# Seven-product blocks in a new order, with two of the sums of each step made by accumulating transfers

## The chip, the cores and the metric

The kernel runs on one core of a Trainium2 chip. The metric is the time of one execution in microseconds on the device; the median of the runs is given. The profile is one execution, taken by the hardware profiler.

## The reference

Two layers work on 256 tokens of width 2048, all in float32. Each layer does, in short:

```
h = rms_norm(x, norm1_g);  z = h @ w_in            # 2048 x 3584: gating u, v; queries, keys, values
A = gating of u by a causal 128 x 128 mixing of v   # 16 channel groups
B = attention in a window of 128, with sinks        # 16 query heads, 4 key/value heads
x = x + concat(rms_norm(A), rms_norm(B)) @ w_out
h2 = rms_norm(x, norm2_g)
x = x + (silu(h2 @ w_gate) * (h2 @ w_up)) @ w_down  # inner width 5632
```

## The kernel before

Every product is made in float32 accuracy from three passes of a faster format: a weight buffer of 128 x 1024 (two slabs of 512 columns, 512 KB, tag `raw`, eight buffers) is loaded from the sync engine's queue, ScalarE casts it to `wh` (five buffers), VectorE makes the remainder `wl = raw - wh` (four buffers), and TensorE multiplies high by high, high by low and low by high (`split2` and `mm3`; lines 123, 124 and 159 to 161). The activations are the stationary side, split once in the same way (`pairs`, `ext`).

An ordinary unit (`unit`) takes one weight buffer to two accumulators of 128 tokens each: twelve matmuls. Most of the feed-forward part's gate and up products (10 of 11 column blocks of 512 in each layer) and the queries are made otherwise, by seven products in place of eight on a 2 x 2 arrangement (`seven`). For the gate and up blocks its rows are the two parities of the inner slabs and its columns are gate and up; for the queries the columns are the two halves. The text writes b11, b12, b21 and b22 for the four weight buffers of a quarter i (i from 0 to 3), and p:i for product p in quarter i: one split and six matmuls into one of five PSUM banks, a half-step. Products 1 and 2 take b11 and b21 plainly; 5 takes b11 + b12, 6 takes b11 + b12 + b22 (`t2`), 3 takes b22, 7 takes b12 + b22, and 4 takes t2 + b21. A block is 28 half-steps.

In the kernel before, the numbers in `bank` are 0 for products 1 and 2, 1 for 5, 3 for 6, 4 for 3 and 2 for 7 and 4. A quarter loads b11, b12 and b22 at once. VectorE adds b12 onto b11 (line 365) and makes t2 (line 366). The sum b12 + b22 is made by VectorE (line 372) or, for the quarters in `by_dma`, by a transfer that GpSimd issues and that adds b22 from memory onto the buffer (line 368). The sum t2 + b21 is always such a transfer (line 374). After the four quarters, bank 0 is copied out and m0 = bank 3 + bank 0 is formed (lines 391 and 392); then come 2:0 to 2:3, with b21 loaded a second time, and 4:0 to 4:3 on the kept t2. Small sums between them (line 396) form c21, c12 and c22, and line 400 puts c21 back into bank 2. `out` then makes the gated activation of each token half (lines 1058 and 1059), which is transposed (`act_T`) for the down product.

The order of the work is the order of the Python calls, with delays counted by `tick`; a planner then orders each engine's instructions and assigns buffers. In the feed-forward part of a layer `s_stream` runs the ten blocks one after the other and yields 300 times (`HALVES`). Beside it, `std_stream` runs ordinary units: 88 of the down product and 16 of the one block that is not done by seven products. Five of them go first (`FF_FIRST`), then they are spread evenly over the yields, and 16 (`TAIL`) remain after the last block. The first layer's queries run beside the key/value, gating and first u products of that layer: `q_to` takes 30 steps of `q["steps"]` in a pace set by the ordinary units; the second layer's run beside the end of the first layer's feed-forward part and the start of the second layer.

Of the kernel before, what the change touches and what calls it, by code (L numbers as in the profile page):

```python
# [12 lines left out]
F32 = mybir.dt.float32  # L13
# [57 lines left out]
EXT_AT = (6.5, 8, 11, 13, 16, 18, 21.5, 24)  # L71
MASK_AFTER = ((5, 5), (4, 4))
GATE_LOAD = ((24, 29), (5, 15))
PARTS = (
    "a0 a0 a1 a1 s a0 a0 s a1 s a1 s s s b0 s b0 s b0 s b0 s b1 s b1 s b1 s b1 s b2 b2 b2 b2 b3 b3 b3 b3",
    "a0 a0 a1 a1 a0 a0 s a1 a1 s b0 b0 s b0 s b0 s s b1 s b1 s b1 s b1 s s b2 s b2 s b2 b2 s b3 b3 b3 b3",
# [14 lines left out]
def trunk(ctx, tc, x, xt, w_in, w_q, w_out, w_oa, w_uh, w_gate, w_up, w_down, sgu_w, sgu_g, consts,  # L91
# [66 lines left out]
    def mm3(acc, ah, al, wh, wl, first, last, again=False):  # L158
        nc.tensor.matmul(acc, ah, wh, start=first, stop=False, skip_group_check=again)  # L159
        nc.tensor.matmul(acc, ah, wl, start=False, stop=False, skip_group_check=again)  # L160
        nc.tensor.matmul(acc, al, wh, start=False, stop=last, skip_group_check=again)  # L161
# [171 lines left out]
    def seven(src, pairs, ext, out, end=lambda sg: None, soon=False, by_dma=(), put_off=False):  # L333
        bank = [pa.tile([P, NB], F32, tag="acc", name=f"m{i}") for i in range(5)]

        def s_unit(raw, m, i, op, first, last):
            wh, wl = split2(raw)
            for j in range(2):
                ah, al = (op(2 * i + j, h) for h in range(2))
                mm3(  # L340
                    bank[m], ah, al, wh[:, j, :], wl[:, j, :], first and j == 0,
                    last and j == 1, m in (0, 2),
                )
            tick(0.5)

        def a_op(k, t):
            return lambda p, h: pairs[p][:, h, k, t * P : (t + 1) * P]

        def e_op(n):
            return lambda p, h: ext[p][:, h, n, :]  # L350

        kept = []
        before = []
        for i in range(4):
            b11 = raw_load(src(0, 0, i))
            b12 = raw_load(src(0, 1, i))
            b22 = raw_load(src(1, 1, i))
            t2 = ap.tile([P, 2, NB], F32, tag="spt", name="t2", bufs=4)
            first, last = i == 0, i == 3
            s_unit(b11, 0, i, a_op(0, 0), first, last)  # L360
            yield
            if soon and first:
                s_unit(b22, 4, i, e_op(3), first, last)
                yield
            nc.vector.tensor_tensor(b11, b11, b12, ALU.add)  # L365
            nc.vector.tensor_tensor(t2, b11, b22, ALU.add)  # L366
            if i in by_dma:
                nc.gpsimd.dma_start(b12, src(1, 1, i), accum_op=ALU.add)
            s_unit(b11, 1, i, e_op(1), first, last)
            yield  # L370
            if i not in by_dma:
                nc.vector.tensor_tensor(b12, b12, b22, ALU.add)
            s_unit(t2, 3, i, e_op(2), first, last)
            anchor[0] = nc.gpsimd.dma_start(t2, src(1, 0, i), accum_op=ALU.add)  # L374
            yield
            if before:
                s_unit(*before.pop())
                yield
            if not (soon and first):
                s_unit(b22, 4, i, e_op(3), first, last)  # L380
                yield
            kept.append(t2)
            if put_off and i in by_dma and not last:
                before.append((b12, 2, i, e_op(0), first, last))
                continue
            s_unit(b12, 2, i, e_op(0), first, last)
            yield
        m0, c12, c21, c22 = (
            zp.tile([P, NB], F32, tag="z", name=v) for v in ("m0", "c12", "c21", "c22")
        )  # L390
        nc.scalar.copy(m0, bank[0])
        nc.vector.tensor_tensor(m0, bank[3], m0, ALU.add)
        yield

        def add(out, x, y):
            nc.vector.tensor_tensor(out, x, y, ALU.add)

        steps = {
            0: lambda: add(c21, bank[2], m0),
            1: lambda: (nc.scalar.copy(bank[2], c21), add(c12, bank[1], m0)),  # L400
            2: lambda: (add(c22, bank[1], c21), add(c12, bank[4], c12)),
            5: lambda: out(0, bank[0], m0, c12),
        }
        for i in range(8):
            if i < 4:
                s_unit(raw_load(src(1, 0, i)), 0, i, a_op(1, 0), False, i == 3)
            else:
                s_unit(kept[i - 4], 2, i - 4, a_op(1, 1), False, i == 7)
            yield
            steps.get(i, lambda: None)()  # L410
        later(1, lambda: out(1, bank[2], c21, c22))
        end([m0, c21])
        yield

    def seven_low(src, pairs, ext, done, tag="hT"):
        def half(raw, acc, op, i, first=False, stop=False):
            wh, wl = split2(raw)
            for j in range(2):
                ah, al = (op(2 * i + j, h) for h in range(2))
                mm3(  # L420
                    acc, ah, al, wh[:, j, :], wl[:, j, :], first and i + j == 0,
                    stop and i + j == 2, not first,
                )
            tick(0.5)

        def a_op(k, t):
            return lambda p, h: pairs[p][:, h, k, t * P : (t + 1) * P]

        def e_op(n):
            return lambda p, h: ext[p][:, h, n, :]  # L430

        def bank(name):
            return pa.tile([P, NB], F32, tag="acc", name=name)

        def held(name):
            return tp.tile([P, 2, NB], F32, tag=tag, name=name)

        x, y, s = [], [], []
        acc0 = bank("l0")
        for i in range(2):  # L440
            x.append(raw_load(src(0, 0, i)))
            y.append(held("ys"))
            nc.sync.dma_start(y[i], src(0, 1, i))
            b22 = raw_load(src(1, 1, i))
            s.append(held("ss"))
            half(x[i], acc0, a_op(0, 0), i, True, True)
            nc.vector.tensor_tensor(x[i], x[i], y[i], ALU.add)
            nc.vector.tensor_tensor(s[i], x[i], b22, ALU.add)
            anchor[0] = nc.gpsimd.dma_start(y[i], src(1, 1, i), accum_op=ALU.add)
            yield  # L450
        acc1 = bank("l1")
        nc.scalar.copy(acc1, acc0)
        for i in range(2):
            half(s[i], acc1, e_op(2), i, False, True)
            anchor[0] = nc.gpsimd.dma_start(s[i], src(1, 0, i), accum_op=ALU.add)
            yield
        mp = wp.tile([P, 2, NB], F32, tag="raw", name="mp", bufs=8)
        nc.scalar.copy(mp[:, 0], acc1)
        acc2 = bank("l2")
        for i in range(2):  # L460
            half(y[i], acc2, e_op(0), i, True, True)
            yield
        nc.scalar.copy(mp[:, 1], acc2)
        for i in range(2):
            half(raw_load(src(1, 0, i)), acc0, a_op(1, 0), i, False, True)
            yield
        done[0, 0](acc0, None)
        for i in range(2):
            half(x[i], acc1, e_op(1), i, False, True)
            yield  # L470
        done[1, 1](acc1, mp[:, 1])
        for i in range(2):
            half(s[i], acc2, a_op(1, 1), i, False, True)
            yield
        done[0, 1](acc2, mp[:, 0])
        for i in range(2):
            half(raw_load(src(1, 1, i)), acc1, e_op(3), i, False, True)
            yield
        done[1, 0](acc1, None)

    def q_product(lay, pairs, ext):
        q = {"k": 0}
        q["steps"] = seven(
            lambda r, c, i: w_q[lay, c, i, r], pairs, ext, lambda *a: q["out"](*a),
            soon=True, by_dma=range(4 if lay == 0 else 0),
        )
        return q

    def q_to(q, share):
# [32 lines left out]
    for lay in range(L):  # L522
# [526 lines left out]
        def act_later(b, sg, held=held, release=release):  # L1049
            for c in range(2):  # L1050
                def ready(c=c):
                    held.append((b, c, sg))
                    release()

                later(2 + c, ready)
# [3 lines left out]
            nc.vector.scalar_tensor_tensor(sg, c, nrstd2[t], sg, ALU.mult, ALU.mult)  # L1059

        def s_block(b, lay=lay, pairs2=pairs2, ext2=ext2, gated=gated, act_later=act_later):
            return seven(
                lambda r, c, i: (w_gate, w_up)[c][lay, b, i, r], pairs2, ext2, gated,
                lambda sg: act_later(b, sg), soon=b == S_BLOCKS[0], by_dma=(0, 2), put_off=True,
            )

        seven_done = [False]

        def s_stream(s_block=s_block):
            for b in S_BLOCKS:  # L1070
                yield from s_block(b)

        seeds = []
        left = [NFF]
# [230 lines left out]
```

## Time and profile before

| | |
|---|---|
| time, median of 3 runs | 1907.09 us (1906.76 to 1910.26) |
| profiled execution | 1906.77 us, its span 1905.1 us |
| TensorE (PE) busy | 1892.9 us, 8624 matmuls and transposes |
| VectorE (DVE) busy | 1745.5 us |
| ScalarE (ACT) busy | 1374.7 us |
| GpSimd (POOL) busy | 183.9 us |
| transfers | 463.12 MB, mean 243 GB/s |

In the profile, a row of a group names the line, the engine, the operation, what is written and what is read with their shapes, the count, the busy time, the mean of one instruction and the idle time of the engine ahead of it with what ended it. PE is the matmuls, PEld the weight loads that run beside them, SPq the sync engine's transfer queue. Matmuls are pipelined and overlap in the record: one lasts 0.39 us, while the next starts earlier.

### The profile page before, as it was taken

The numbers are of one execution on the slowest core, as the hardware profiler recorded it, in microseconds if no ns is written. First come the engines' busy times: TensorE is split into PE (matmuls) and PEld (weight loads), VectorE is DVE, ScalarE is ACT, GpSimd is POOL, SyncE is SP. The second block draws the span as 40 slices with busy tenths as digits, with TensorE's granted clock in tenths as the row PEclk, the third lists the DMA queues.
The fourth block names the chain that finished last, engine by engine and source line by source line (L and its number), as shares of the span: only waits on it lengthen the run. The fifth ranks groups of instructions, "written<-read, shape, count | busy, mean of one in ns | idle before, by whom it ended". The sixth has DMA issues, their size and how long they took to land.

```text
span 1905.1 us, 25218 instructions
## 1 busy us (share of the span) xinstructions
PE 1892.9 (99%) x8624; PEld 1544.2 (81%) x8624; DVE 1745.5 (92%) x1894; ACT 1374.7 (72%) x1860; POOL 183.9 (10%) x184
## 2 busy tenths in 40 slices
PE   9999999999999999999999999999999999999999
PEld 6887788888888888888888778888888888888887
DVE  7988989999999999999798888999999999999993
ACT  8668777677767776777776886766877677676774
POOL 0231001000100001000002200000000100010000
PEclk9999999999999999999999999999999999999999
DMA  9973668888977897889578648697789788888783
GB/s 356 261 284 133 194 202 243 248 247 276 271 238 245 270 290 228 243 261 290 185 217 291 191 153 237 212 280 224 233 282 288 227 254 264 270 249 251 249 277 110
DMA packets 129153, 463.12 MB, mean 243 GB/s; under 512 B 14336, under 2 KB 14720, under 8 KB 129024
## 3 DMA queue, kind: packets, MB, share of 16 engines
q1 hardware_dynamic: 105840, 378.54, 53.9%
q0 software_dynamic: 22464, 81.80, 23.7%
q8 instruction: 67, 1.10, 0.2%
q10 hardware_dynamic: 720, 1.18, 0.2%
q14 instruction: 62, 0.51, 0.1%
HBM read 459.36 MB, written 2.10 MB: 242 GB/s over the span
## 4 chain that ended last, share of the span: by engine, by line
PE 94%; ACT 2%; DVE 2%; issue 1%; DMA 0%; POOL 0%; SPq 0%; DVEq 0%; ACTq 0%; POOLq 0%
PE m L160 15%; PE m L159 15%; PE m L161 15%; PE dacc L160 11%; PE dacc L159 11%; PE dacc L161 11%; PE acc L160 4%; PE acc L161 3%; PE acc L159 3%; PE l L159 1%; PE l L160 1%; PE l L161 1%; PE ps_f L242 1%; PE ps_n L242 1%; DVE wl L124 1%
## 5 line engine op out<-in xcount | busy, mean ns | idle before, releaser
L123 ACT CAST wh<-raw 128x1024 fp32r<-128x1024 f32 (+1 forms) x794 | 814.0, 1050 | 366.5 <-DVE raw L365 165.7
L124 DVE TENSOR_TENSOR wl<-raw,wh 128x1024 fp32r<-128x1024 f32 (+1 forms) x794 | 943.9, 1217 | 83.0 <-issue 25.5
L159 PE MATMUL m<-wh,ext 128*128 128x512 f32 x704 | 276.7, 393 | 0.0
L160 PE MATMUL m<-wl,ext 128*128 128x512 f32 x704 | 275.0, 391 | 0.0
L161 PE MATMUL m<-wh,ext 128*128 128x512 f32 x704 | 274.4, 390 | 0.0
L160 PE MATMUL dacc<-wl,aT 128*128 128x512 f32 x624 | 243.5, 390 | 0.0
L159 PE MATMUL dacc<-wh,aT 128*128 128x512 f32 x624 | 243.0, 391 | 0.0
L161 PE MATMUL dacc<-wh,aT 128*128 128x512 f32 x624 | 242.9, 389 | 0.0
L124 DVE TENSOR_TENSOR wl<-t,wh 128x1024 fp32r<-128x1024 f32 x176 | 213.1, 1221 | 10.0 <-issue 5.2
L123 ACT CAST wh<-t 128x1024 fp32r<-128x1024 f32 x176 | 184.3, 1051 | 37.0 <-DVE t L366 14.1
L159 PE MATMUL m<-wh,hT 128*128 128x512 f32 x528 | 206.3, 391 | 0.0
L160 PE MATMUL m<-wl,hT 128*128 128x512 f32 x528 | 205.7, 390 | 0.0
L161 PE MATMUL m<-wh,hT 128*128 128x512 f32 x528 | 205.5, 389 | 0.0
L160 PEld LDWEIGHTS m<-wl,ext 128*128 128x128 f32 x704 | 132.2, 188 | 29.1 <-DVE wl L124 2.2
L159 PEld LDWEIGHTS m<-wh,ext 128*128 128x128 f32 x704 | 132.2, 188 | 27.6 <-ACT wh L123 0.8
L161 PEld LDWEIGHTS m<-wh,ext 128*128 128x128 f32 x704 | 132.1, 188 | 27.5
L159 PEld LDWEIGHTS dacc<-wh,aT 128*128 128x128 f32 x624 | 117.1, 188 | 25.0 <-ACT wh L123 0.7
L160 PEld LDWEIGHTS dacc<-wl,aT 128*128 128x128 f32 x624 | 117.2, 188 | 24.7 <-DVE wl L124 0.6
L161 PEld LDWEIGHTS dacc<-wh,aT 128*128 128x128 f32 x624 | 117.1, 188 | 24.2
L374 POOL DMA_DIRECT2D t<-in_w_gate_dram x80 | 69.1, 864 | 525.0 <-DVE wl L124 412.9
L161 PEld LDWEIGHTS m<-wh,hT 128*128 128x128 f32 x528 | 99.1, 188 | 20.6
L159 PEld LDWEIGHTS m<-wh,hT 128*128 128x128 f32 x528 | 99.1, 188 | 20.3
(212 smaller groups left out, 2907.5 us busy)
## 6 DMA issues: line engine op xcount, KB each, us to landing
raw<-in_w_gate_dram SPq DMA_DIRECT2D x176, 512.0 KB, 5.9
raw<-in_w_up_dram SPq DMA_DIRECT2D x176, 512.0 KB, 5.9
raw<-in_w_down_dram SPq DMA_DIRECT2D x176, 512.0 KB, 5.8
t<-in_w_gate_dram POOLq DMA_DIRECT2D x80, 512.0 KB, 7.7
raw<-in_w_in_dram SPq DMA_DIRECT2D x68, 512.0 KB, 6.7
raw<-in_w_out_dram SPq DMA_DIRECT2D x48, 512.0 KB, 4.3
raw<-in_w_up_dram POOLq DMA_DIRECT2D x40, 512.0 KB, 6.5
raw<-in_w_q_dram SPq DMA_DIRECT2D x32, 512.0 KB, 5.7
```

The source lines that it names most:

```text
L123: nc.scalar.copy(wh[:, j : j + step, :], src)
L124: last_wl[0] = nc.vector.tensor_tensor(wl[:, j : j + step, :], src, f(wh[:, j : j + step, :]), ALU.subtract)
L159: nc.tensor.matmul(acc, ah, wh, start=first, stop=False, skip_group_check=again)
L160: nc.tensor.matmul(acc, ah, wl, start=False, stop=False, skip_group_check=again)
L161: nc.tensor.matmul(acc, al, wh, start=False, stop=last, skip_group_check=again)
L242: nc.tensor.transpose(ps[:, j, t * P : (t + 1) * P], blocks[t][:, j * P : (j + 1) * P], ident)
L374: anchor[0] = nc.gpsimd.dma_start(t2, src(1, 0, i), accum_op=ALU.add)
```

## The change

The new class `Lean` replaces `seven` in the feed-forward part of both layers and in the first layer's queries; the second layer's queries keep `seven`. A block has the same 28 half-steps. What differs:

- b12 isn't loaded. It is added by a transfer onto b11's buffer once product 1 has split it (`one`), and onto b22's buffer once product 3 has split it and t2 is formed (`five`). Both transfers are issued by GpSimd.
- t2 is formed by VectorE from the two buffers (b11 + b12, and b22), and b21 is added to it by VectorE in `two`, from the one load that product 2 uses as well.
- Bank 0 is copied into bank 3 ahead of product 6, which accumulates onto it; m0 is then a copy of bank 3.
- The half-steps follow a written order (`LEAN`, for the queries `LEAN_Q`): products 1, 3, 5, 7 and 6 of different quarters are interleaved, then come 2:0 to 2:3 and 4:0 to 4:3. The first two half-steps of a block (1:0 and 3:0) stand among product 4 of the block before.
- Each half-step loads its own buffer; before, a quarter's three loads were called together.

```diff
+LEAN_END = " 2:0 2:1 2:2 2:3 4:0 4:1 4:2 4:3"
+LEAN = "1:0 3:0 1:1 5:0 3:1 1:2 3:2 5:1 7:0 1:3 5:2 3:3 7:1 6:0 5:3 6:1 7:2 6:2 6:3 7:3" + LEAN_END
+LEAN_Q = "1:0 3:0 1:1 5:0 3:1 1:2 5:1 7:0 3:2 1:3 5:2 7:1 6:0 3:3 5:3 6:1 7:2 6:2 6:3 7:3" + LEAN_END
...
+    class Lean:
...
+            self.home = {
+                1: (0, a_op(0, 0)), 2: (0, a_op(1, 0)), 3: (4, e_op(3)), 4: (2, a_op(1, 1)),
+                5: (1, e_op(1)), 6: (3, e_op(2)), 7: (2, e_op(0)),
+            }
...
+        def onto(self, dst, i):
+            anchor[0] = nc.gpsimd.dma_start(dst, self.src(0, 1, i), accum_op=ALU.add)
+
+        def one(self, i):
+            self.raw[1, i] = raw_load(self.src(0, 0, i))
+            self.half(1, self.raw[1, i], i)
+            self.onto(self.raw[1, i], i)
+
+        def three(self, i):
+            self.raw[3, i] = raw_load(self.src(1, 1, i))
+            self.half(3, self.raw[3, i], i)
+
+        def five(self, i):
+            self.half(5, self.raw[1, i], i)
+            self.t2[i] = ap.tile([P, 2, NB], F32, tag="spt", name="t2", bufs=4)
+            self.add(self.t2[i], self.raw[1, i], self.raw[3, i])
+            self.onto(self.raw[3, i], i)
+
+        def six(self, i):
+            if i == 0:
+                nc.scalar.copy(self.acc(3), self.bank[0])
+            self.half(6, self.t2[i], i)
+
+        def seven(self, i):
+            self.half(7, self.raw[3, i], i)
+
+        def two(self, i):
+            b21 = raw_load(self.src(1, 0, i))
+            self.half(2, b21, i)
+            self.add(self.t2[i], self.t2[i], b21)
+            z, bank = self.z, self.bank
+            if i == 0:
+                for v in ("m0", "c12", "c21", "c22"):
+                    z[v] = zp.tile([P, NB], F32, tag="z", name=v)
+                nc.scalar.copy(z["m0"], bank[3])
+            elif i == 1:
+                self.add(z["c21"], bank[2], z["m0"])
+            elif i == 2:
+                nc.scalar.copy(bank[2], z["c21"])
+                self.add(z["c12"], bank[1], z["m0"])
+            else:
+                self.add(z["c22"], bank[1], z["c21"])
+                self.add(z["c12"], bank[4], z["c12"])
+
+        def four(self, i):
+            self.half(4, self.t2[i], i)
+            z, bank = self.z, self.bank
+            if i == 0:
+                self.out(0, bank[0], z["m0"], z["c12"])
+            elif i == 3:
+                later(1, lambda: self.out(1, bank[2], z["c21"], z["c22"]))
+                self.end([z["m0"], z["c21"]])
+
+    def lean_run(blocks, order=LEAN):
+        steps = []
+        for n, b in enumerate(blocks):
+            for at, name in enumerate(order.split()):
+                steps.append((28 * n + (at if at > 1 else (-4.5, -2.5)[at]), n, at, b, name))
...
+            yield
+            if name in ("6:3", "4:3"):
+                yield
...
-        q["steps"] = seven(
-            lambda r, c, i: w_q[lay, c, i, r], pairs, ext, lambda *a: q["out"](*a),
-            soon=True, by_dma=range(4 if lay == 0 else 0),
-        )
+        args = (lambda r, c, i: w_q[lay, c, i, r], pairs, ext, lambda *a: q["out"](*a))
+        q["steps"] = lean_run([Lean(*args)], LEAN_Q) if lay == 0 else seven(*args, soon=True)
...
-            return seven(
+            return Lean(
                 lambda r, c, i: (w_gate, w_up)[c][lay, b, i, r], pairs2, ext2, gated,
-                lambda sg: act_later(b, sg), soon=b == S_BLOCKS[0], by_dma=(0, 2), put_off=True,
+                lambda sg: act_later(b, sg),
             )
...
-            for b in S_BLOCKS:
-                yield from s_block(b)
+            return lean_run([s_block(b) for b in S_BLOCKS])
```

More of the change, by code (lines that the diff above doesn't have):

```diff
@@ L413, in seven, with __init__, a_op, e_op @@
         yield
+    class Lean:
+        def __init__(self, src, pairs, ext, out, end=lambda sg: None):
+            self.src, self.out, self.end = src, out, end
+            self.bank, self.raw, self.t2, self.z = {}, {}, {}, {}
+            def a_op(k, t):
+                return lambda p, h: pairs[p][:, h, k, t * P : (t + 1) * P]
+            def e_op(n):
+                return lambda p, h: ext[p][:, h, n, :]
+            self.home = {
+                1: (0, a_op(0, 0)), 2: (0, a_op(1, 0)), 3: (4, e_op(3)), 4: (2, a_op(1, 1)),
+                5: (1, e_op(1)), 6: (3, e_op(2)), 7: (2, e_op(0)),
+            }
+        def acc(self, m):
+            if m not in self.bank:
+                self.bank[m] = pa.tile([P, NB], F32, tag="acc", name=f"m{m}")
+            return self.bank[m]
+        def half(self, n, raw, i):
+            m, op = self.home[n]
+            wh, wl = split2(raw)
+            first, last = n in (1, 3, 5, 7) and i == 0, i == 3
+            for j in range(2):
+                ah, al = (op(2 * i + j, h) for h in range(2))
+                mm3(
+                    self.acc(m), ah, al, wh[:, j, :], wl[:, j, :], first and j == 0,
+                    last and j == 1, m in (0, 2, 3),
+                )
+            tick(0.5)
+        def add(self, out, x, y):
+            nc.vector.tensor_tensor(out, x, y, ALU.add)
+        def onto(self, dst, i):
[43 more added lines that the diff above has]
+                self.end([z["m0"], z["c21"]])
@@ new lines, in lean_run @@
+    def lean_run(blocks, order=LEAN):
[3 more added lines that the diff above has]
+                steps.append((28 * n + (at if at > 1 else (-4.5, -2.5)[at]), n, at, b, name))
+        for _, _, _, b, name in sorted(steps, key=lambda e: e[:3]):
+            {
+                "1": b.one, "2": b.two, "3": b.three, "4": b.four, "5": b.five, "6": b.six,
+                "7": b.seven,
+            }[name[0]](int(name[2]))
+            yield
+            if name in ("6:3", "4:3"):
+                yield
```

## The prediction

> **What bounds the kernel now.** I read the page's busy times and its chain first.
>
> ```profile
> span 1905.1 us, 25218 instructions
> PE 1892.9 (99%) x8624; PEld 1544.2 (81%) x8624; DVE 1745.5 (92%) x1894; ACT 1374.7 (72%) x1860; POOL 183.9 (10%) x184
> PE 94%; ACT 2%; DVE 2%; issue 1%; DMA 0%; POOL 0%; SPq 0%; DVEq 0%; ACTq 0%; POOLq 0%
> ```
>
> The chain that ended last is 94% matmul. VectorE, at 92%, has 2% of it. But matmuls overlap, so a busy PE does not prove that no slot is lost. The starts of neighbouring matmuls tell that (timeline of PE in the feed-forward part).
>
> ```profile
> 599.84 0.39 PE L161 MATMUL m<-wh,hT 128*128 128x512 f32 x1
> ...
> 608.00 0.39 PE L161 MATMUL dacc<-wh,aT 128*128 128x512 f32 x1
> ...
> 608.34 0.27 PE L242 MATMUL ps_f<-ident,c 128*128 128x128 f32 x1
> 608.44 0.27 PE L242 MATMUL ps_f<-ident,m 128*128 128x128 f32 x1
> ```
>
> Between the first two rows lie 36 starts in 8.16 us: a 512-column matmul starts every 0.227 us, and a transpose (the last two) every 0.11. Next the stretches that hold little but feed-forward work, all instructions first, then the transposes alone.
>
> ```profile
> 400.00:900.00 500.00, 500.00 (x2231) 412.03 (x2230) 480.59 (x450) 357.79 (x416) 41.49 (x48) 1.00 0.84 259
> 1300.00:1850.00 550.00, 550.00 (x2457) 452.80 (x2456) 529.90 (x497) 394.83 (x461) 45.84 (x53) 1.00 0.85 260
> 400.00:900.00 500.00, 9.71 (x64) 7.71 (x64) 10.94 (x16) 9.36 (x16) 1.00 0.84 259
> 1300.00:1850.00 550.00, 12.14 (x80) 9.61 (x80) 13.66 (x20) 11.68 (x20) 1.00 0.85 260
> ```
>
> Columns: stretch, length, busy PE, PEld, DVE, ACT, POOL (in the last two rows no POOL), granted clock, DMA share, GB/s. In the first stretch 2231 - 64 = 2167 matmuls x 0.2267 + 64 x 0.11 = 498.3 of 500 us; in the second 2377 x 0.2267 + 80 x 0.11 = 547.7 of 550. So TensorE loses 4.0 us in 1050, at a full clock, while DVE is at 96%. Little can be won here. What ends the waits that are there is told by the waits of the weight loads, in the same two stretches:
>
> ```profile
> PEld m L160 <- DVE wl L124: 1.0, 4, 0.4
> PEld m L159 <- ACT wh L123: 0.3, 1, 0.3
> PEld dacc L160 <- DVE wl L124: 0.3, 1, 0.3
> ...
> PEld m L160 <- DVE wl L124: 0.8, 3, 0.4
> PEld m L159 <- ACT wh L123: 0.5, 2, 0.3
> PEld dacc L159 <- ACT wh L123: 0.4, 1, 0.4
> PEld dacc L160 <- DVE wl L124: 0.3, 1, 0.3
> ```
>
> Splits that came late cost 1.6 and 2.0 us: 3.6 us in 1050. Scaled to the two feed-forward parts (about 1340 us, from 300 to 965 and from 1228 to 1900) that is 4.6 us. This is the most that a lighter VectorE can give back there.
>
> **The change part by part.** A block is 28 half-steps of six matmuls before and after, as many transposes follow it, and the stream still yields 30 times a block. So TensorE's work is the same: 0.
>
> *VectorE and ScalarE.* Prices, from the groups (line, engine, operation, count | busy, mean ns of one | idle before):
>
> ```profile
> L124 DVE TENSOR_TENSOR wl<-raw,wh 128x1024 fp32r<-128x1024 f32 x790 | 941.3, 1220 | 82.2 <-issue 25.5 <-ACT wh L123 23.2 <-PE acc L160 13.3
> L123 ACT CAST wh<-raw 128x1024 fp32r<-128x1024 f32 x790 | 811.6, 1052 | 366.3 <-DVE raw L365 165.7 <-PE dacc L161 87.4 <-PE acc L161 36.1
> L372 DVE TENSOR_TENSOR raw<-raw 128x1024 f32<-128x1024 f32 x44 | 53.6, 1218 | 0.0
> L392 DVE TENSOR_TENSOR m<-m,m 128x512 f32<-128x512 f32 x22 | 15.1, 685 | 1.3 <-PE m L161 1.2
> L391 ACT COPY m<-m 128x512 f32<-128x512 f32 x22 | 12.7, 576 | 0.0
> ```
>
> Ten sums a feed-forward block become eight: 20 blocks x 2 x 1.22 = 48.8 us less DVE. The first layer's queries had eight and keep eight. The sum m3 + m0 goes in 21 blocks (the second layer's queries stay as they are): 21 x 0.685 = 14.4 us. It becomes a copy of bank 0 into bank 3 ahead of product 6: 21 x 0.58 = 12 us more on ACT. All of it lies beside TensorE: DVE goes from 1745 to about 1682 us, ACT to 1387. On the path is only what removes late splits: between 0 and 4.6 us. I take half, 2.3 us, since new waits (below) will make some splits late again.
>
> *Transfers.* A feed-forward block goes from 16 loads and 6 accumulating transfers to 12 and 8; the first layer's queries from 16 and 8 to 12 and 8.
>
> ```profile
> q1 hardware_dynamic: 105840, 378.54, 53.9%
> q0 software_dynamic: 22464, 81.80, 23.7%
> raw<-in_w_gate_dram SPq DMA_DIRECT2D x176, 512.0 KB, 5.9
> ss<-in_w_oa_dram POOLq DMA_DIRECT2D x4, 512.0 KB, 9.6
> L368 POOL DMA_DIRECT2D raw<-in_w_up_dram x40: 863/863/910, 286.7 to 1816.4; - x40
> DMA to landing us min/median/max: 5.2/6.4/8.8
> DMA to landing us min/median/max: 5.6/7.6/10.3
> ACT wh L123: 0.5, 1
> ```
>
> (The two landing rows are those of the sums b12 + b22 and t2 + b21; the last row is who waited for the former: once, 0.5 us.) A load takes 0.539 x 1905.1 / 378.54 x 0.524 MB = 1.42 us of all 16 engines, a transfer of the software queue 0.237 x 1905.1 / 81.8 x 0.524 = 2.89. A block then needs 16 x 1.42 + 6 x 2.89 = 40.1 us before and 12 x 1.42 + 8 x 2.89 = 40.2 after: nothing won, nothing lost on the mean. In the queries 4 x 1.42 = 5.7 us of transfer time go, but SP's loads are ahead of TensorE there:
>
> ```profile
> 14.00:50.00 36.00, 35.72 (x156) 29.28 (x157) 31.46 (x48) 32.06 (x57) 3.53 (x3) 1.00 1.02 372
> PEld acc L160 <- DVE wl L124: 0.7, 1, 0.7
> PEld dacc L160 <- DVE wl L124: 0.4, 1, 0.4
> ```
>
> Though the DMA engines are full from 14 to 50 us, TensorE waits for splits only 1.1 us between 14 and 150 us (the two wait rows). The queries' part is worth 0 to 1.1 us; I take 0.
>
> *The new wait.* This is the real risk. Product 1 of a quarter is split from b11, then b12 is added onto the same buffer by a transfer, and the cast for product 5 must wait for its landing. Product 7's buffer is made likewise after product 5. In the new order the distance is mostly five half-steps (1:1 to 5:1, 5:1 to 7:1, 1:3 to 5:3, 5:3 to 7:3). Between the half-steps run ordinary units of twelve matmuls: of a layer's 104, 5 come first and 16 are left for the end, so 83 over 300 yields, 0.277 each. So a step is 6 x 0.227 + 0.277 x 12 x 0.227 = 2.1 us of TensorE, and five are 10.6. The link needs a landing, a cast and a subtraction: 7.6 + 1.05 + 1.22 = 9.9 us with the slower median, 8.7 with the faster. It fits, with 0.7 us to spare. Behind a late cast on ACT stand all later casts, the copies out of PSUM and the Silu; DVE's subtraction waits for the cast, and TensorE for both. How far they may fall back is shown by ACT where it is as far ahead as it may be:
>
> ```profile
> 1403.00 1.06 ACT L123 CAST wh<-raw 128x1024 fp32r<-128x1024 f32 x1 [0.30 <-PE m L161]
> 1404.36 1.05 ACT L123 CAST wh<-raw 128x1024 fp32r<-128x1024 f32 x1 [0.30 <-PE m L161]
> 1436.81 5.81 DVE L124 TENSOR_TENSOR wl<-raw,wh 128x1024 fp32r<-128x1024 f32 x5
> ```
>
> A cast starts when TensorE frees the fifth buffer back; four units are then ahead, at least 4 x 1.36 = 5.4 us, less 1.05 and 1.22: a lead of about 3.2 us. Five subtractions on end took 5.81 us, 1.16 each. Bounds of this wait: 0 (the landing stays under 10.6 - 2.3 = 8.3 us) and 2.8 us a block, 56 us in all (three links in a row, 1:1 to 5:1 and then 1:3 to 5:3 to 7:3, at the longest landing of 10.3 us: 3 x 2.0 less the lead). A gain is excluded: before, nobody waited for these transfers. I take 0, since both medians are under 8.3 us.
>
> The Trainium skill, "DMA: Bandwidth & Descriptors", Anatomy of one DMA, gives 2.0 us plus bytes over 436 GB/s for such a transfer: 3.2 us here, as an estimate from that page. By it the link would take 5.5 us and this wait could not arise; the traces show 6.4 and 7.6, so the measurement decides and the risk stands. A rule that speaks against the change is in "SBUF — State Buffer", the trap of DVE blocking DMA: GpSimd may be locked out of writing descriptors by VectorE. POOL's issues took 863 to 910 ns beside a DVE at 96%, so no run here shows it, and two more a block should not.
>
> *Queues and banks.* POOL issues eight instead of six a block, in order, each behind a subtraction: at 0.86 us and 10% busy, 0. SP's loads are issued a step at a time, not three at once; at the fullest place (3:2) five of the eight buffers hold sums under way, so three loads are on their way, 5.9 us each, where 0.95 load a step of 2.1 us needs 2.7. It fits barely: 0, or one step of 2.1 us that the lead covers. The next block's first two half-steps move in among product 4's. They need two banks, and those of products 6, 5 and 3 are read out by 2:3: 0. In the queries the extended activations are wanted earlier (3:3 as fourteenth step), just after they are made: 0, at most one wait of about 2 us.
>
> **The sum.** 1905.1 - 2.3 = 1902.8 us of span. The profiled execution took 1906.77, 1.7 over its span, and the median is 1907.09, 0.3 above that: 1904.8, so about 1905.
>
> **The rivals.** *The landing comes late (slower).* From 1:1 to 7:3 the new order packs seven accumulating transfers, 7 x 2.89 = 20.2 us of all engines, and with some ten loads (14.2 us) 34 us into 17 steps of 2.1 us = 36 us: nearly full, so landings stretch. For it: the row of 9.6 us, where two accumulating transfers stood close. Against: fewer loads compete. It decides above 8.3 us. At 9.6 a link takes 11.9 us, 1.3 too many; three links 3.9, less the lead 3.2: 0.7 x 20 blocks = 14 us, so 1921. Sharing of engines is also what the Trainium skill's section "Issuing engines are not separate DMA queues" on the same DMA page says, and no run here shows it alone.
>
> *VectorE's sums in a row (slower).* Steps 2:0 to 2:3 each carry a sum, and four small ones of 0.68 besides: 4 x (1.16 + 1.16 + 0.277 x 1.16) + 4 x 0.68 = 13.3 us of DVE against 4 x 2.1 = 8.4 of TensorE: 4.9 behind, 1.7 more than the lead, x 20 = 34 us: 1939. It decides when the written order holds on DVE. Against: the operands of these sums are there earlier, so they may be placed in DVE's pauses before.
>
> *All late splits vanish (faster).* With 63 us off DVE and the DMA relief at the start: 4.6 + 1.1 = 5.7 us: 1901. For it: most of those waits name DVE. Against: ACT's are among them, and it gains a copy and the new waits.
>
> *Nothing moves.* The wait rows are then the pipeline's own small change: 1907; this is one with my forecast by measure.
>
> **How the numbers follow.** What a measurement of this kernel can tell from no change is about 0.2%, 3.8 us: 1903.3 to 1910.9. My forecast with its neighbour "nothing moves" has 0.54 (own range 1903 to 1909), all splits vanish 0.18, late landing 0.17, sums in a row 0.11. Faster 0.18, same 0.54, slower 0.28. The range goes from 1900 to 1930: below it is left what would win more than all the late splits (0.04), above it the dearer third of the late landing (0.06) and nearly all of the sums in a row (0.1), 0.2 together.
>
> **What would show it.** Right: DVE near 1682 us, the sum lines 40 fewer in the feed-forward part, 84 loads fewer on SP and 40 more issues on POOL, PE's starts still 0.227 us apart, PEld's waits for splits under 3 us. Wrong: landings of the accumulating transfers above 8.3 us with ACT's casts waiting for DMA (late landing); PEld waiting for wl at product 2, once a block, for 1 to 2 us (sums in a row). Any new gap on PE of over 0.2 us that comes back every 62 us would break the forecast.

## The result, and the profile after

The changed kernel takes 2146.09 us (median of 5 runs, 2136.97 to 2146.69), the kernel before 1908.77 us in the same comparison: a ratio of 1.1233, with an interval of 1.1211 to 1.1256. It is 12% slower, where the prediction said 1905 us and a range of 1900 to 1930. The profiled execution took 2146.69 us.

The page of the changed kernel: span, busy times, the two queues, and the lines of the busy digits for TensorE and its clock.

```profile
span 2145.0 us, 25278 instructions
PE 1971.1 (92%) x8624; PEld 1584.7 (74%) x8624; DVE 1679.6 (78%) x1833; ACT 1403.4 (65%) x1881; POOL 210.5 (10%) x224
PE   9899998899889989998999999888999799899999
PEclk9999998999999999999999999999999899999999
q1 hardware_dynamic: 93744, 334.49, 44.4%
q0 software_dynamic: 28224, 102.77, 26.8%
```

The work is what was counted: as many matmuls, VectorE at 1679.6 us (1682 was forecast), 105840 - 93744 = 12096 packets of the sync queue fewer, which is 84 loads of 144 packets, and 224 - 184 = 40 issues more on GpSimd. But TensorE stands idle for 2145.0 - 1971.1 = 174 us, where it had been 12 (1905.1 - 1892.9). The two feed-forward stretches of the prediction, all instructions (columns as there):

```profile
400.00:900.00 500.00, 446.75 (x1885) 359.94 (x1884) 384.98 (x362) 313.11 (x360) 46.68 (x54) 0.96 0.74 203
1300.00:1850.00 550.00, 492.06 (x2081) 397.48 (x2079) 417.96 (x422) 342.30 (x411) 49.78 (x57) 0.95 0.74 202
```

1885 matmuls and transposes in 500 us, where there were 2231; VectorE does 385 us in place of 481, so it is not short of time. The granted clock is 0.96 and 0.95, not 1.00. Who waits, from the waits of the whole span (engine, tile and line, what ended the wait: us in total, times, the longest; line 126 is the cast, 127 the subtraction, 163 the matmuls with `wl`, 452 the big sums, 455 the issue of the transfers that add b12), and the group of the sum t2:

```profile
DVE t L452 <- DMA raw<-in_w_up_dram: 302.5, 70, 7.3
ACT wh L126 <- DMA raw<-in_w_up_dram: 111.8, 36, 6.0
PEld m L163 <- DVE wl L127: 95.9, 41, 6.1
PE m L163 <- DVE wl L127: 79.9, 32, 5.7
PE dacc L163 <- DVE wl L127: 36.4, 18, 5.3
L452 DVE TENSOR_TENSOR t<-raw 128x1024 f32<-128x1024 f32 x84 | 102.9, 1225 | 314.8 <-DMA raw<-in_w_up_dram 302.5 <-DMA raw<-in_w_q_dram 9.1 <-issue 3.2
```

The first row is the finding. (b22, a load of the sync queue, comes from the same tensor; but the view of line 455 names the waiting sums too, and these wait for the transfers of b12 alone.)

```profile
  DVE t L452: 311.6, 74
  ACT wh L126: 111.8, 36
```

In 74 of its 84 places, four of them in the queries, the sum t2 = (b11 + b12) + b22 stops VectorE until the transfer of b12 has landed, 4.2 us on the mean and 7.3 at most. In the kernel before, the views of the two adding transfers (lines 368 and 374) name one waiter in all, a cast for 0.5 us, and no VectorE instruction. How one of these waits reaches TensorE is to be read in 20 us of the three engines' timelines (start, duration, engine, line, operation; in brackets the idle time ahead and what ended it). VectorE, then GpSimd, then TensorE:

```profile
1659.28 1.22 DVE L127 TENSOR_TENSOR wl<-t,wh 128x1024 fp32r<-128x1024 f32 x1
1660.41 3.49 DVE L127 TENSOR_TENSOR wl<-raw,wh 128x1024 fp32r<-128x1024 f32 x3
1671.06 1.23 DVE L452 TENSOR_TENSOR t<-raw 128x1024 f32<-128x1024 f32 x1 [7.16 <-DMA raw<-in_w_up_dram]
1672.20 0.75 DVE L1163 SCALAR_TENSOR_TENSOR c<-c,nr,c 128x512 f32<-128x512 f32 x1
1672.87 4.63 DVE L127 TENSOR_TENSOR wl<-raw,wh 128x1024 fp32r<-128x1024 f32 x4
```

```profile
1661.92 0.86 POOL L455 DMA_DIRECT2D raw<-in_w_up_dram  x1 [3.29 <-DVE wl L127]
```

```profile
1668.84 0.39 PE L164 MATMUL m<-wh,ext 128*128 128x512 f32 x1
1669.07 0.27 PE L245 MATMUL ps_f<-ident,m 128*128 128x128 f32 x1
1673.01 0.48 PE L245 MATMUL ps_f<-ident,c 128*128 128x128 f32 x1 [3.67 <-DVE c L1163]
...
1675.16 0.63 PE L162 MATMUL m<-wh,ext 128*128 128x512 f32 x1
...
1677.72 0.63 PE L162 MATMUL m<-wh,hT 128*128 128x512 f32 x1
...
1678.55 0.40 PE L164 MATMUL m<-wh,hT 128*128 128x512 f32 x1
```

A subtraction of product 1 ends, GpSimd issues the transfer at 1661.92, and VectorE reaches the sum at 1663.90, two subtractions later. The transfer lands at about 1671. For 7.16 us VectorE does nothing, and behind the sum stand a gating operation and four subtractions, none of which needs the transfer. TensorE uses up what lay ready, and stops for 3.67 us at a transpose whose operand VectorE should have made. After that its matmuls start slower: between the rows at 1675.16 and 1677.72 lie six starts, 0.427 us each in place of 0.227. Over the span I count 247 starts of 512-column matmuls at this slower pace, which lose 49 us, and 106 gaps of 0.46 us and more, which lose 179 us; before, it was 7 (1.3 us) and 12 (6.1 us). That accounts for 220 of the 240 us by which the span grew.

### The profile page after: what moved, and what is told of

Its sections match the earlier page's. It is cut to its first block, busy times and chain, and to the rows that moved or that the text cites. A ratio compares the mean times of both kernels' runs of the same rounds, so it can differ in the third digit from the quotient of the medians.

```text
span 2145.0 us, 25278 instructions
## 1 busy us (share of the span) xinstructions
PE 1971.1 (92%) x8624; PEld 1584.7 (74%) x8624; DVE 1679.6 (78%) x1833; ACT 1403.4 (65%) x1881; POOL 210.5 (10%) x224
## 3 DMA queue, kind: packets, MB, share of 16 engines
q1 hardware_dynamic: 93744, 334.49, 44.4%
## 5 line engine op out<-in xcount | busy, mean ns | idle before, releaser
L163 PE MATMUL m<-wl,ext 128*128 128x512 f32 x704 | 290.7, 413 | 65.5 <-DVE wl L127 65.4
L452 DVE TENSOR_TENSOR t<-raw 128x1024 f32<-128x1024 f32 x84 | 102.9, 1225 | 314.8 <-DMA raw<-in_w_up_dram 302.5
L162 PE MATMUL m<-wh,ext 128*128 128x512 f32 x704 | 288.6, 410 | 0.0
L164 PE MATMUL m<-wh,ext 128*128 128x512 f32 x704 | 286.7, 407 | 0.0
L163 PE MATMUL dacc<-wl,aT 128*128 128x512 f32 x624 | 252.9, 405 | 36.4 <-DVE wl L127 36.4
L455 POOL DMA_DIRECT2D raw<-in_w_up_dram x160 | 138.5, 866 | 1271.2 <-DVE wl L127 598.0
L162 PE MATMUL dacc<-wh,aT 128*128 128x512 f32 x624 | 252.7, 405 | 0.0
L164 PE MATMUL dacc<-wh,aT 128*128 128x512 f32 x624 | 250.2, 401 | 0.0
L163 PEld LDWEIGHTS m<-wl,ext 128*128 128x128 f32 x704 | 139.9, 199 | 105.7 <-DVE wl L127 77.3
L164 PEld LDWEIGHTS m<-wh,ext 128*128 128x128 f32 x704 | 139.6, 198 | 29.2
L162 PEld LDWEIGHTS m<-wh,ext 128*128 128x128 f32 x704 | 139.4, 198 | 29.4
L162 PEld LDWEIGHTS dacc<-wh,aT 128*128 128x128 f32 x624 | 121.7, 195 | 26.1 <-ACT dacc L1211 0.6
L164 PEld LDWEIGHTS dacc<-wh,aT 128*128 128x128 f32 x624 | 121.8, 195 | 25.6
L163 PEld LDWEIGHTS m<-wl,hT 128*128 128x128 f32 x528 | 101.1, 191 | 39.5 <-DVE wl L127 18.6
```

The source lines that it names most:

```text
L455: anchor[0] = nc.gpsimd.dma_start(dst, self.src(0, 1, i), accum_op=ALU.add)
```

## The experiments

Theory A: a planner orders each engine's instructions, and it places the sum t2 where it takes the transfer to have landed (what it reckons with is an assumption; its places are read from the trace). In the written order t2 stands behind product 5's subtraction. In VectorE's order as built, all 84 stand ahead of it by 2 to 11 instructions, and only 3 to 16 (median 5) behind the subtraction of product 1 that lets the transfer be issued. Theory B: the chain from product 1 to product 5 and on to 7 is too short for the landing in any case, by the cast that waits. The rest were aimed at the two parts of the change and at the length of the transfer.

**The sum t2 pinned to its written place (`pin`).**

```diff
-            self.add(self.t2[i], self.raw[1, i], self.raw[3, i])
+            with tc.issue_after(last_wl[0].ins):
+                self.add(self.t2[i], self.raw[1, i], self.raw[3, i])
```

> The changed kernel, with one edit: the sum t2 = (b11+b12) + b22 must stand on VectorE behind product 5's subtraction of the same quarter, where the program text puts it; in the changed kernel it stands up to four subtractions earlier. Theory A (VectorE stops at this sum, since the planner put it soon after the transfer it waits for, and everything behind it on VectorE stops with it): the sum's waits for transfers fall from 302 us to under 30, and the time to 1905 to 1935 us. Theory B (five half-steps are too short for a landing, wherever the sum stands): the wait moves to ScalarE's cast for product 5 and the time stays over 2050. Theory C (the accumulating transfers load the DMA engines too much): no change, 2130 to 2150.

1978.6 us, 1.0374 (1.0344 to 1.0404). 71 us are lost in place of 237. Its waits:

```profile
ACT wh L126 <- DMA raw<-in_w_up_dram: 151.9, 74, 6.1
DVE wl L127 <- ACT wh L126: 99.4, 102, 3.8
DVE t L452 <- DMA raw<-in_w_gate_dram: 44.5, 14, 5.7
DMA to landing us min/median/max: 5.1/8.1/11.7
```

The waits of t2 for its transfer are gone, and with them two thirds of the loss, so the early sum is a cause and theory C is out. But the time lies between the ranges of theory A (1935 us or less) and theory B (over 2050). Theory B's wait came up in its place: 74 casts now wait for the landing, where it was 36 in the changed kernel. And the second sum, t2 + b21, waits for a load of b21 for the same reason as the first (placed early).

**The two parts by themselves: only the feed-forward part (`ff_only`), only the queries (`q_only`).** One of the two goes back to `seven`.

```diff
-        q["steps"] = lean_run([Lean(*args)], LEAN_Q) if lay == 0 else seven(*args, soon=True)
+        q["steps"] = seven(*args, soon=True, by_dma=range(4 if lay == 0 else 0))
```

> The changed kernel with the first layer's queries made as before the change; the feed-forward part stays changed. The last query work in the first layer ends some 15 us later in the changed kernel (first ps_v transpose product at 187.1 instead of 172.1 us). If that is the queries' whole share, this kernel takes about 2131 us; if their delay was hidden later, 2146.

> The complement: only the first layer's queries in the new way, the feed-forward part as before. All theories: 1909 + 15 = about 1924 us if the parts add up. With the run that has the feed-forward part alone this says whether the two shares add.

2140.6 us (1.1222, 1.1198 to 1.1246) and 1919.5 us (1.0063, 1.0041 to 1.0084). So the feed-forward part costs 233 us and the queries 12, each by its own; the sum of 245 is 8 above the 237 of both, hardly more than the three intervals leave open (4 to 5 us each). In the queries the sums wait 6 times in 8 (4 times t2 for its transfer, twice the second sum for b21; VectorE's waits from 14 to 160 us in the kernel with the queries alone, then the stretch from 50 to 100 us of that kernel, then that of the kernel before):

```profile
DVE t L452 <- DMA raw<-in_w_q_dram: 11.8, 6, 4.0
```

```profile
50.00:100.00 50.00, 42.58 (x183) 33.53 (x181) 38.62 (x50) 31.34 (x39) 10.58 (x11) 1.00 0.81 236
```

```profile
50.00:100.00 50.00, 50.00 (x222) 41.32 (x222) 46.24 (x55) 34.75 (x42) 9.69 (x8) 1.00 0.91 265
```

39 matmuls fewer in these 50 us are 8.9 us at 0.227 us each, most of the 12.

**A longer distance, with t2 pinned (`far_pin`).** Products 5 and 7 follow six to nine half-steps behind their transfers in the block's list (seven to twelve with the half-steps of the neighbouring blocks that stand between), in place of mostly five, and three half-steps stand ahead among the block before.

```diff
-LEAN = "1:0 3:0 1:1 5:0 3:1 1:2 3:2 5:1 7:0 1:3 5:2 3:3 7:1 6:0 5:3 6:1 7:2 6:2 6:3 7:3" + LEAN_END
+LEAN = "1:0 1:1 3:0 1:2 1:3 3:1 5:0 5:1 3:2 6:0 6:1 5:2 3:3 5:3 7:0 7:1 6:2 6:3 7:2 2:0 7:3 2:1 2:2 2:3 4:0 4:1 4:2 4:3"
...
-                steps.append((28 * n + (at if at > 1 else (-4.5, -2.5)[at]), n, at, b, name))
+                steps.append((28 * n + (at if at > 2 or order != LEAN else (-6.5, -4.5, -2.5)[at]), n, at, b, name))
```

> As the pinned kernel, and in the feed-forward part the half-steps in another written order, so that product 5 follows product 1 and product 7 follows product 5 of the same quarter by seven to eleven half-steps in place of five (one step of the next block more stands among the tail of the block before). Theory A: what the pin left is small, so this differs from the pinned kernel by under 15 us. Theory B: the pinned kernel is still far too slow and this one is over 100 us faster than it. If raw buffers held longer starve the loads, it is slower than the pinned kernel, with SP's loads as the late releaser.

1951.3 us, 1.0235 (1.0205 to 1.0265). What VectorE waits for now:

```profile
DVE t L452 <- DMA raw<-in_w_gate_dram: 68.9, 32, 4.6
```

That is 27 us less than with `pin`, between what the two theories gave (under 15 and over 100). Casts hardly wait for the transfers any more (4 times, 3.4 us); the second sum does wait, 32 times, for b21. It was not pinned.

**Both sums pinned, in the order of the change (`pin2`) and in the far order (`far_pin2`); the far order with none pinned (`far_free`).** The second pin, for the sum t2 + b21:

```diff
-            self.add(self.t2[i], self.t2[i], b21)
+            with tc.issue_after(last_wl[0].ins):
+                self.add(self.t2[i], self.t2[i], b21)
```

> The pinned kernel, with the second sum of a quarter (t2 + b21, in product 2's step) pinned as well, behind product 2's subtraction. In the pinned kernel (1979 us) VectorE still waits 44.5 us at this sum for b21's load, and ScalarE 152 us at product 5's and 7's casts for landings (median 8.1 us). Theory A: only the 44.5 us go, of which TensorE sees a part: 1950 to 1972. The rest is theory B's: it stays.

> The kernel with the far order, both sums pinned. With the far order ScalarE's waits for landings were 3.4 us, with 68.9 us of VectorE's waits at t2 + b21 left and TensorE 43 us late. Theory A (every sum that the planner puts ahead of its transfer stops VectorE; distance cures the rest): 1903 to 1918. If the four sums in a row of product 2 or late loads cost as much by themselves, it stays at 1935 to 1955.

> The far order without any pin: the planner is free to put the sums where it thinks their transfers have landed. Theory A: the distance does not help VectorE, since the sum follows its transfer and not its step; over 2050 us, with some 200 us or more of VectorE's waits for transfers at the sums. Theory B (distance alone is the matter): 1935 to 1965, like the pinned far order.

| time lost against the kernel before, us (ratio, interval) | sums placed by the planner | both sums pinned |
|---|---|---|
| order of the change | 237.3 (1.1233, 1.1211 to 1.1256) | 56.2 (1.0289, 1.0275 to 1.0304) |
| far order | 115.1 (1.0605, 1.0586 to 1.0624) | -1.7 (0.9991, 0.9982 to 1.0000) |

With both pinned, in the order of the change, the waits of ACT and VectorE are these, and, from the view of line 455, who waited for the adding transfers and how long they took:

```profile
ACT wh L126 <- DMA raw<-in_w_up_dram: 155.8, 79, 4.8
DVE wl L127 <- ACT wh L126: 150.6, 133, 4.4
  ACT wh L126: 157.1, 80
DMA to landing us min/median/max: 5.2/8.0/11.5
```

Both runs with pins came out in the ranges expected (1964.7 and 1906.7 us). In the order of the change no sum waits for a transfer any more; what is left, 56 us, goes with the casts' wait for the landing. With the far order and no pin both sums wait (the third row is again from the view of line 455: who waited for the adding transfers):

```profile
DVE t L452 <- DMA raw<-in_w_up_dram: 100.6, 45, 5.8
DVE t L452 <- DMA raw<-in_w_gate_dram: 66.5, 40, 4.3
  DVE t L452: 59.9, 22
```

Of these 167 us only 60 are for the adding transfers; the rest are for loads of b22 and b21 that had not come either when the early sum was reached. The time, 2023.6 us, lies between the ranges of the two theories. Theory A's ground, that the sum follows its transfer and not its step, holds only in part: in the order as built the sum t2 stands median 9 instructions behind product 1's subtraction, where it was 5 in the order of the change, and 22 of 84 wait for their transfer, where it was 74. With both, the far order and the pins, the page, the first stretch, the cast's wait and the landing are:

```profile
PE 1890.1 (99%) x8624; PEld 1545.1 (81%) x8624; DVE 1683.8 (88%) x1833; ACT 1402.0 (74%) x1881; POOL 218.2 (11%) x224
400.00:900.00 500.00, 498.30 (x2227) 411.54 (x2226) 454.98 (x425) 368.23 (x423) 55.36 (x64) 1.00 0.87 241
ACT wh L126 <- DMA raw<-in_w_up_dram: 15.8, 11, 2.9
DMA to landing us min/median/max: 5.1/7.7/11.2
```

TensorE is back at 2227 matmuls in the stretch and at a full clock, while the transfers land as slowly as ever (7.7 us). So the loss is in where the waits stand, not in the transfers or the number of issues. Each of the two causes costs by itself: measured from this last kernel, early sums cost 117 us in the far order and the short distance 58 with the sums pinned. Together they cost 239, which is 64 more than their sum. Two things go that way: the short distance puts the early sums nearer to their transfers (5 instructions in place of 9), and the stops are long enough that TensorE slows down behind more of them. By the count of slow starts above, these lose 49 us with both causes, 28 with the early sums alone and 2 to 3 with the short distance alone, so about 20 of the 64 us.

**The far order, both pins, and `seven` for the queries (`far_pin2_ff`).** The edit for the queries is that of `ff_only`.

> As the far order with both sums pinned, with the first layer's queries as before the change. The queries' part cost 12 us alone and unpinned; pinned, the mark at the end of the first layer's attention stood 5 us later than in the kernel before. So 5 us less than the run beside it: 1898 to 1913.

1908.74 us, 1.0003 (0.9994 to 1.0012). That is 2.0 us more than with the new queries, not the 5 less that I had expected, though inside the range given. The two intervals overlap, so the comparison does not tell whether the new queries, once pinned, gain anything.

**Copying in place of adding transfers (`plain_pin2`, `plain_free`).** b12 is copied onto the buffer, so that the sums b11 + b12 and b12 + b22 are left out. In the traces every engine has the same instructions in the same order as in `pin2` and in the changed kernel respectively; only the transfer is another.

```diff
-            anchor[0] = nc.gpsimd.dma_start(dst, self.src(0, 1, i), accum_op=ALU.add)
+            anchor[0] = nc.gpsimd.dma_start(dst, self.src(0, 1, i))
```

> The changed order with both sums pinned behind the subtraction written ahead of them, and the transfers of b12 only copy instead of adding (the sums b11 + b12 and b12 + b22 are left out, so the products 5, 6, 7 and 4 are of other numbers). The same instructions on every engine. Theory A (what is left of the loss, 56 us, is the link's length): loads from SP of the same size land in 4.3 to 5.9 us, so the link shrinks by some 2 to 3.5 us under the 8.0 us of the adding transfers and fits in five half-steps; 1905 to 1920 us, and the casts' waits for the transfer fall from 156 us to under 25. Theory B (the order itself costs, by its banks or its loads): above 1945 us, with waits that do not name the transfer.

> The changed kernel as it is, with copying transfers in place of adding ones (the same sums left out). Theory A (the early sum stands behind the transfer by 3 to 16 instructions of VectorE, whatever the landing is): a landing shorter by 2 to 3.5 us takes that much off each of some 70 waits of 4.3 us and most of the casts': 1940 to 2030 us. Theory B (the number of early sums costs, not how long they wait): above 2080 us.

1913.0 us (1.0026, 1.0016 to 1.0036) and 1942.8 us (1.0180, 1.0164 to 1.0195), both as theory A gave. The landing with the sums pinned, then the landing and two waits with the sums placed by the planner:

```profile
DMA to landing us min/median/max: 3.4/4.8/7.8
```

```profile
DMA to landing us min/median/max: 3.4/4.2/8.0
DVE t L452 <- DMA raw<-in_w_up_dram: 103.1, 49, 5.2
ACT wh L126 <- DMA raw<-in_w_up_dram: 26.5, 18, 4.0
```

A landing shorter by 3.2 us takes 51 of the 56 us away with the sums pinned, in the order of the change (3 casts wait for the transfer, 2.2 us in all): the distance of five half-steps is right for a landing of 4.8 us and wrong for one of 8.0. With the sums placed by the planner, 2.8 us less of landing saves 202 of 237 us: VectorE still waits 49 times, 2.1 us each, but only 35 us of it reach the end: that a short wait fits into what TensorE has in hand is how I read it.

## Why the prediction was wrong

- **What bounds the kernel, and the counts: right.** TensorE had no slack, VectorE came to 1679.6 us against 1682, the packets and issues are as counted. ACT came to 1403 against 1387, off the path. Whether the gain of 2.3 us from late splits is there stays open: with the far order and both pins the kernel is 1.7 us faster (0.9982 to 1.0000), at the edge of what can be told.
- **The new wait: the step that failed.** It named the cast for product 5 as the one that waits for the landing, and priced it. It did not ask which other instruction reads the buffer. That is the sum t2 on VectorE, which reads b11 + b12 too. The prediction does not name it, as if it stood where it is written, behind product 5's subtraction, though the front text says that a planner orders each engine; it stands median 5 instructions behind the subtraction that lets the transfer go. This term was 0 in the sum and measured 181 us in the order of the change (237.3 with the planner's places, 56.2 with the written ones): 166 of them by t2 (71.0 are left when it alone is pinned), the other 15 by the second sum, pinned after it, which the planner had put ahead of the load of b21.
- **The same step, its second half: mis-sized.** The cast's wait was priced at 0, "since both medians are under 8.3 us". With the sums pinned it costs 56 us. That this is also the upper bound of the prediction is luck: the bound took three links at 10.3 us in every block, while `pin2` has 80 waits of 2.0 us on the mean and landings of up to 11.5 us. Two things were off. First, the median is the wrong measure: it was 8.0 us, under the limit of 8.3, and still 69 of the 168 transfers landed later than 8.3. Second, the link to product 7 holds more than a landing, a cast and a subtraction: its transfer is issued only behind the sum t2, which the prediction left out here too. In the trace of `pin2`, matched to the half-steps by the written order, that transfer is issued 1.43 us (median) behind product 5's subtraction and lands in 8.6 us; the one for product 5 is issued 0.29 us behind product 1's and lands in 6.9. With the cast and the subtraction (1.05 and 1.22 us) these are 12.3 and 9.4 us, where 10.6 were reckoned for five half-steps. So 59 of the waits, 126 of the 157 us, are product 7's. In the changed kernel, where t2 stands early and frees that transfer early, all 36 waiting casts are product 5's.
- **"The landing comes late": not the main cause, and too cheap for the rest.** In the changed kernel landings took 7.0 us in the median, between the 6.4 and 7.6 of before, so they were not stretched. With the sums pinned they took 8.0, and the casts then wait for them as this rival says, but for 56 us where it gave 14.
- **"VectorE's sums in a row": the sign was wrong.** It took the written order for the danger and the earlier place for the cure ("they may be placed in DVE's pauses before"). With both sums held in their written places and a far enough distance nothing is lost, and `plain_pin2`, which keeps the order of the change with its four sums in a row, loses 5.6 us in all, where this rival gave 34. The earlier place is what stopped VectorE. (The 1939 us of this rival add its 34 to the forecast of 1905, while the 1921 of the rival before add 14 to 1907.)
- **What would show it.** "Any new gap on PE" was there. The predicted sign for a late landing, ACT's casts waiting for DMA, was there in 36 places, but the larger row was one that the prediction had not thought of: DVE waiting for DMA.

Behind the gap of 3.67 us six starts took 0.427 us each, and the granted clock from 1671.7 to 1678.5 us is 0.50. The prediction priced stalls as lost slots alone; 49 of the 240 us are starts at this pace. The Trainium skill's page "TensorE: Matmul & The Clock Gate", HAM oscillation, says that TensorE's clock drops to half when it is idle for longer than about 3.4 us. The half clock agrees with this trace, the length only in part: of the 31 stretches at a granted clock of 0.5 in the changed kernel's span, 14 stand behind a gap of over 3.4 us, and 17 behind shorter ones, the longest gap in the 9 us ahead being 1.8 to 3.3 us.

## What to carry to other kernels

Where a transfer takes the place of a sum, list every instruction that reads the buffer, on every engine, and look up where the planner puts each in its engine's order: an engine that runs in order turns one early reader into a stop for everything behind it. Put such a reader behind work that needs no transfer, and give the link the length of the longest landing, not of the median. Look as well for what a moved instruction releases: the sum that waits here also lets the next transfer go, so holding it back makes the next link longer. When a wait of 2 us or more reaches TensorE, count the slower matmuls behind it too.

## What the runs showed of the hardware

The same instructions with an adding transfer of 512 KB land in 8.0 us in the median (5.2 at least), with a copying one in 4.8 (3.4 at least). The Trainium skill's "DMA: Bandwidth & Descriptors", Anatomy of one DMA, leads to 3.2 us for this size, as estimated in the prediction: that is near the shortest copy here (3.4 us) and far from the adding transfer, beside which the prediction had set it. GpSimd's issue also differs: the first row is the adding one (both sums pinned), the second the copying one.

```profile
L455 POOL DMA_DIRECT2D raw<-in_w_up_dram x160: 857/863/910, 285.3 to 1882.9; - x160
```

```profile
L455 POOL DMA_DIRECT2D raw<-in_w_up_dram x160: 527/537/602, 286.6 to 1829.9; - x160
```

What stays open is the rest of what the two causes cost together beyond their sum, some 44 of 64 us, and whether the 8 us by which the two parts of the change cost more apart than together are more than noise.
